# A mixture-of-experts dispatch on one core: loads and stores in one queue, larger transfers, and one broadcast multiply per token

## The chip, the cores and the metric

The kernel runs on one core of a Trainium2 chip. The metric is the device time of one execution in microseconds; lower is better. The kernel before takes 94.59 us (median of 3 runs, 94.53 to 94.8). The span in the profile is shorter, 92.7 us, because it begins with the first and ends with the last recorded instruction.

## The reference

For each of 8 x 256 = 2048 tokens there are a vector x of 512 numbers and 8 gate weights. The weights are divided by their sum, and the output holds x eight times, once per expert, multiplied by that expert's weight:

```
x            [8, 256, 512]     float32
gate_weights [8, 256, 8]       float32
gate_weights = gate_weights / (sum(gate_weights, axis=-1) + 1e-8)
output       [8, 256, 8, 512]  = x[:, :, None, :] * gate_weights[:, :, :, None]
```

The input is 4.26 MB and the output 33.55 MB.

## The kernel before, in words

The 2048 tokens lie over P = 128 partitions, J = 16 consecutive tokens to a partition. One token's output is E x D = 8 x 512 numbers, 16 KB in a partition, and what one partition stores for m tokens is one contiguous run of m x 16 KB in memory.

**Loads.** All gate weights go to `g_all` in one transfer (L54, SyncE's queue). x goes to one tile, `x_all`, in three transfers: tokens 0 and 1 (L55, ScalarE's queue), tokens 2 to 8 (L56, SyncE's queue) and tokens 9 to 15 (L57, ScalarE's queue). No input is loaded later.

**Weights.** VectorE sums the eight weights of each token (L64), takes the reciprocal (L66; the 1e-8 is left out) and multiplies (L68, the reciprocal broadcast over the experts). The result is `gn`. A small copy on ScalarE (L61) brings in its function table early.

**Multiplies.** `compute_tile` (L72) fills one output tile for m tokens with 8 x m multiplies of 128x512 each, one per token and expert. The first `ACT_SHARE[m]` of them go to ScalarE (6 of 16 for two tokens, 10 of 24 for three; L46), the rest to VectorE (L49).

**Stores.** The 16 tokens go in tiles of 2, 3, 3, 3, 3 and 2. The first tile is stored from SyncE's queue (L84), the others from ScalarE's (L89 and L94), so ScalarE's program holds both multiplies and stores, in order. The last 16 numbers of each partition are copied to a small tile `sent` (L100) and stored from SyncE's queue (L101).

**Buffers and order.** The tile pool has three buffers, so the fourth tile waits until the first store has landed, the fifth for the second, and the sixth for the third. The order on each engine is the order of the program; a framework adds the waits for data and for buffers.

Of the kernel before, what the change touches and what calls it, by code (L numbers as in the profile page):

```python
# [1 line left out]

# [4 lines left out]

ACT_SHARE = {1: 3, 2: 6, 3: 10, 4: 13}
SENT = 16  # L10


@with_exitstack
def kernel(
    ctx: ExitStack,
    tc: tile.TileContext,
    x: bass.AP,
    gate_weights: bass.AP,
    out: bass.AP,
):  # L20
    nc = tc.nc
    P = 128

    B, S, D = x.shape
    E = gate_weights.shape[-1]
    n_tok = B * S
    J = n_tok // P

    fp32 = mybir.dt.float32

    x_v = x.flatten_outer_dims().rearrange("(p j) d -> p j d", p=P)
    g_v = gate_weights.flatten_outer_dims().rearrange("(p j) e -> p j e", p=P)
    out_v = out.rearrange("b s e d -> (b s) e d").rearrange(
        "(p j) e d -> p j e d", p=P
    )
    out_flat = out.rearrange("b s e d -> (b s) (e d)").rearrange(
        "(p j) q -> p (j q)", p=P
    )
    tokq = E * D

    xpool = ctx.enter_context(tc.tile_pool(name="xpool", bufs=1))
    gpool = ctx.enter_context(tc.tile_pool(name="gpool", bufs=1))
    tpool = ctx.enter_context(tc.tile_pool(name="tpool", bufs=3))

    def mul_scalar(o_ap, x_ap, s_ap):
        nc.scalar.mul(out=o_ap, in_=x_ap, mul=s_ap)  # L46

    def mul_vector(o_ap, x_ap, s_ap):
        nc.vector.tensor_scalar_mul(out=o_ap, in0=x_ap, scalar1=s_ap)  # L49

    g_all = gpool.tile([P, J, E], fp32)
    x_all = xpool.tile([P, J, D], fp32)

    nc.sync.dma_start(out=g_all, in_=g_v)  # L54
    nc.scalar.dma_start(out=x_all[:, 0:2, :], in_=x_v[:, 0:2, :])  # L55
    nc.sync.dma_start(out=x_all[:, 2:9, :], in_=x_v[:, 2:9, :])  # L56
    nc.scalar.dma_start(out=x_all[:, 9:J, :], in_=x_v[:, 9:J, :])  # L57

    warm = gpool.tile([P, 1], fp32)
    nc.vector.memset(warm, 0.0)  # L60
    nc.scalar.copy(out=warm, in_=warm)  # L61

    gsum = gpool.tile([P, J, 1], fp32)
    nc.vector.reduce_sum(out=gsum, in_=g_all, axis=mybir.AxisListType.X)  # L64
    rsum = gpool.tile([P, J, 1], fp32)
    nc.vector.reciprocal(out=rsum, in_=gsum)  # L66
    gn = gpool.tile([P, J, E], fp32)
    nc.vector.tensor_tensor(  # L68
        out=gn, in0=g_all, in1=rsum.to_broadcast([P, J, E]), op=mybir.AluOpType.mult
    )  # L70

    def compute_tile(pool, j0, m):  # L72
        o_tile = pool.tile([P, m, E, D], fp32)
        n_act = ACT_SHARE[m]
        k = 0
        for jj in range(m):
            for e in range(E):
                mul = mul_scalar if k < n_act else mul_vector
                mul(o_tile[:, jj, e, :], x_all[:, j0 + jj, :], gn[:, j0 + jj, e : e + 1])
                k += 1  # L80
        return o_tile

    tile_p0 = compute_tile(tpool, 0, 2)
    nc.sync.dma_start(out=out_v[:, 0:2, :, :], in_=tile_p0)  # L84

    for t in range(4):
        j0 = 2 + 3 * t
        o_tile = compute_tile(tpool, j0, 3)
        nc.scalar.dma_start(out=out_v[:, j0 : j0 + 3, :, :], in_=o_tile)  # L89

    j0 = J - 2
    last_tile = compute_tile(tpool, j0, 2)
    lf = last_tile.rearrange("p a e d -> p (a e d)")
    nc.scalar.dma_start(  # L94
        out=out_flat[:, j0 * tokq : J * tokq - SENT],
        in_=lf[:, 0 : 2 * tokq - SENT],
    )

    sent = gpool.tile([P, SENT], fp32)
    nc.scalar.copy(out=sent, in_=lf[:, 2 * tokq - SENT : 2 * tokq])  # L100
    nc.sync.dma_start(out=out_flat[:, J * tokq - SENT : J * tokq], in_=sent)  # L101


# [1 line left out]
_INS = ['x', 'gate_weights']  # L105
_OUTS = [((8, 256, 8, 512), 'float32')]


# [23 lines left out]
```

## Time and profile before

| | |
|---|---|
| time | 94.59 us (94.53 to 94.8) |
| span | 92.7 us |
| VectorE busy | 31.4 us, 34% of the span |
| ScalarE busy | 34.0 us, 37% of the span |
| read from HBM, written | 4.26 MB, 33.55 MB |
| mean rate over the span | 408 GB/s |
| one multiply on ScalarE, on VectorE | 707 ns, 480 ns |

Times are in us from the start of the span. In the lines of the profile, DVE is VectorE, ACT is ScalarE, POOL is GpSimd and SP is SyncE; a name with a q behind it (SPq, ACTq) is that engine's sequencer, which issues transfers. L49 is line 49 of the kernel. A row of 40 digits shows the busy share of 40 equal slices of the span in tenths. In groups, `o_tile<-x_all,gn` says what is written and what is read, x76 how often.

### The profile page before, as it was taken

Reading aid. Unit: us, or ns where it says so; the run is one execution under the profiler, and the core shown is the slowest. Engines: PE = TensorE matmul, PEld = TensorE weight load, DVE = VectorE, ACT = ScalarE, POOL = GpSimd, SP = SyncE. Lnnn points to the kernel's source line nnn. Section 1 sums busy time; section 2 is a strip of 40 time slices with the busy share of each in tenths; the row PEclk is TensorE's granted clock in tenths of the full one; section 3 lists DMA queues with packets and bytes.
Section 4 is the critical chain, followed back from the end, with each engine's and each line's share of the span. In section 5 each row is a group of like instructions: output and inputs, shape, how many; then the busy total and the mean of one; then the engine's idle time right before and its main releaser. Section 6 shows DMA issues by size and latency. Waiting matters only on the chain.

```text
span 92.7 us, 204 instructions
## 1 busy us (share of the span) xinstructions
DVE 31.4 (34%) x80; ACT 34.0 (37%) x55; POOL 0.2 (0%) x4
## 2 busy tenths in 40 slices
DVE  0199008999999300399000097000000000000000
ACT  2378008999999910399200096000000000000000
POOL 0000000000000000000000000000000000000000
DMA  1999999999879989988998898899889988999980
GB/s 23 423 402 451 414 350 438 452 452 537 382 339 551 445 360 403 572 382 343 509 466 382 382 572 360 385 445 531 361 361 531 446 382 360 487 451 409 409 367 0
DMA packets 1586, 37.83 MB, mean 408 GB/s; under 512 B 304, under 2 KB 432, under 8 KB 560
## 3 DMA queue, kind: packets, MB, share of 16 engines
q10 hardware_dynamic: 1008, 31.71, 79.8%
q1 hardware_dynamic: 576, 6.10, 15.9%
q14 instruction: 2, 0.02, 0.0%
HBM read 4.26 MB, written 33.55 MB: 408 GB/s over the span
## 4 chain that ended last, share of the span: by engine, by line
DMA 43%; ACT 12%; DVE 4%; issue 1%; DVEq 0%; SPq 0%
DMA out_dram<-o_tile 29%; DMA x_all<-in_x_dram 14%; ACT o_tile L46 12%; DVE o_tile L49 4%; DVEq L127 0%; SPq L54 0%; ACT sent L100 0%; DVEq L49 0%
## 5 line engine op out<-in xcount | busy, mean ns | idle before, releaser
L46 ACT ACTIVATE o_tile<-x_all,gn 128x512 f32<-128x512 f32 x52 | 32.3, 707 | 21.6 <-DMA out_dram<-o_tile 14.3
L49 DVE TENSOR_SCALAR o_tile<-x_all,gn 128x512 f32<-128x512 f32 x76 | 30.5, 480 | 21.8 <-DMA out_dram<-o_tile 16.7
L61 ACT ACT_TABLE_LOAD x1 | 1.3, 1283 | 1.6 <-PEq L116 1.6
L64 DVE TENSOR_REDUCE gsum<-g_all 128x16 f32<-128x128 f32 x1 | 0.3, 286 | 3.4 <-DMA g_all<-in_gate_weights_dram 3.4
L100 ACT COPY sent<-o_tile 128x16 f32<-128x16 f32 x1 | 0.2, 204 | 0.4 <-DVE o_tile L49 0.4
L60 DVE MEMSET warm<- 128x1 f32 x1 | 0.1, 59 | 0.8 <-PEq L116 0.8
L68 DVE TENSOR_TENSOR gn<-g_all,rsum 128x128 f32<-128x128 f32 x1 | 0.3, 293 | 0.0
L66 DVE RECIPROCAL rsum<-gsum 128x16 f32<-128x16 f32 x1 | 0.3, 253 | 0.0
L61 ACT COPY warm<-warm 128x1 f32<-128x1 f32 x1 | 0.2, 191 | 0.0
L116 POOL MEMSET const-bfloat16-1.0<- 128x1 bf16 x1 | 0.1, 102 | 0.0
L116 POOL MEMSET const-uint8-127<- 128x1 uint8 x1 | 0.1, 102 | 0.0
L116 POOL MEMSET const-float32-0.0<- 128x1 f32 x1 | 0.1, 99 | 0.2 <-issue 0.2
L116 POOL MEMSET const-float32-1.0<- 128x1 f32 x1 | 0.1, 99 | 0.0
## 6 DMA issues: line engine op xcount, KB each, us to landing
out_dram<-o_tile ACTq DMA_DIRECT2D x4, 6144.0 KB, 27.8
out_dram<-o_tile SPq DMA_DIRECT2D x1, 4096.0 KB, 14.7
out_dram<-o_tile ACTq DMA_DIRECT2D x1, 4088.0 KB, 34.4
x_all<-in_x_dram ACTq DMA_DIRECT2D x1, 1792.0 KB, 13.2
x_all<-in_x_dram SPq DMA_DIRECT2D x1, 1792.0 KB, 13.0
x_all<-in_x_dram ACTq DMA_DIRECT2D x1, 512.0 KB, 3.9
g_all<-in_gate_weights_dram SPq DMA_DIRECT2D x1, 64.0 KB, 3.5
out_dram<-sent SPq DMA_DIRECT2D x1, 8.0 KB, 18.6
```

Of the source, the lines that this page charges most:

```text
L46: nc.scalar.mul(out=o_ap, in_=x_ap, mul=s_ap)
L49: nc.vector.tensor_scalar_mul(out=o_ap, in0=x_ap, scalar1=s_ap)
L60: nc.vector.memset(warm, 0.0)
L61: nc.scalar.copy(out=warm, in_=warm)
L64: nc.vector.reduce_sum(out=gsum, in_=g_all, axis=mybir.AxisListType.X)
L66: nc.vector.reciprocal(out=rsum, in_=gsum)
L68: nc.vector.tensor_tensor(out=gn, in0=g_all, in1=rsum.to_broadcast([P, J, E]), op=mybir.AluOpType.mult)
L100: nc.scalar.copy(out=sent, in_=lf[:, 2 * tokq - SENT : 2 * tokq])
L116: nc = _bacc.Bacc("TRN2", target_bir_lowering=False, num_devices=1)
```

## The change

It brings the work into one buffer and one queue:

- **Queues.** `g_all` is loaded from ScalarE's queue, and x from SyncE's in two transfers (5 and 11 tokens instead of 2, 7 and 7). All stores are issued from SyncE's queue, so that ScalarE's program holds no store.
- **Larger transfers.** The tokens go in chunks of 2, 3, 3, 4 and 4 (`CHUNKS`: first token, number of tokens, first slot), five stores instead of six. The split-off of the last 16 numbers is dropped.
- **Ten token slots.** In place of three buffers there is one tile `ring` with ten slots of one token each. Chunks 1 to 3 take slots 0-1, 2-4 and 5-7; chunk 4 takes slots 0-3, and chunk 5 slots 6-9. Slots 8 and 9 are used only once.
- **Multiplies.** Tokens 0 and 1 are split as before, three experts of each on ScalarE and five on VectorE. From token 2 on, the first token of each chunk is ScalarE's (eight multiplies), and each other token is one `tensor_tensor` on VectorE over 8 x 512 elements, with x broadcast over the experts and the weights over the 512 elements (`scale_token`).
- **1e-8.** It is added to the sum with one more operation on VectorE, as in the reference.

```diff
--- before.py
+++ after.py
@@ -1,4 +1,3 @@
-
 from contextlib import ExitStack
 
 import concourse.bass as bass
@@ -6,8 +5,9 @@
 from concourse import bass_utils, mybir
 from concourse._compat import with_exitstack
 
-ACT_SHARE = {1: 3, 2: 6, 3: 10, 4: 13}
-SENT = 16
+SLOTS = 10
+HEAD = 5
+CHUNKS = ((0, 2, 0), (2, 3, 2), (5, 3, 5), (8, 4, 0), (12, 4, 6))
 
 
 @with_exitstack
@@ -23,82 +23,70 @@
 
     B, S, D = x.shape
     E = gate_weights.shape[-1]
-    n_tok = B * S
-    J = n_tok // P
+    J = B * S // P
 
     fp32 = mybir.dt.float32
+    mult = mybir.AluOpType.mult
 
     x_v = x.flatten_outer_dims().rearrange("(p j) d -> p j d", p=P)
     g_v = gate_weights.flatten_outer_dims().rearrange("(p j) e -> p j e", p=P)
     out_v = out.rearrange("b s e d -> (b s) e d").rearrange(
         "(p j) e d -> p j e d", p=P
     )
-    out_flat = out.rearrange("b s e d -> (b s) (e d)").rearrange(
-        "(p j) q -> p (j q)", p=P
-    )
-    tokq = E * D
 
-    xpool = ctx.enter_context(tc.tile_pool(name="xpool", bufs=1))
-    gpool = ctx.enter_context(tc.tile_pool(name="gpool", bufs=1))
-    tpool = ctx.enter_context(tc.tile_pool(name="tpool", bufs=3))
+    pool = ctx.enter_context(tc.tile_pool(name="pool", bufs=1))
 
-    def mul_scalar(o_ap, x_ap, s_ap):
-        nc.scalar.mul(out=o_ap, in_=x_ap, mul=s_ap)
+    g_all = pool.tile([P, J, E], fp32)
+    x_all = pool.tile([P, J, D], fp32)
+    ring = pool.tile([P, SLOTS, E, D], fp32)
+    gsum = pool.tile([P, J, 1], fp32)
+    gn = pool.tile([P, J, E], fp32)
+    warm = pool.tile([P, 1], fp32)
 
-    def mul_vector(o_ap, x_ap, s_ap):
-        nc.vector.tensor_scalar_mul(out=o_ap, in0=x_ap, scalar1=s_ap)
+    nc.scalar.dma_start(out=g_all, in_=g_v)
+    nc.sync.dma_start(out=x_all[:, 0:HEAD, :], in_=x_v[:, 0:HEAD, :])
+    nc.sync.dma_start(out=x_all[:, HEAD:J, :], in_=x_v[:, HEAD:J, :])
 
-    g_all = gpool.tile([P, J, E], fp32)
-    x_all = xpool.tile([P, J, D], fp32)
-
-    nc.sync.dma_start(out=g_all, in_=g_v)
-    nc.scalar.dma_start(out=x_all[:, 0:2, :], in_=x_v[:, 0:2, :])
-    nc.sync.dma_start(out=x_all[:, 2:9, :], in_=x_v[:, 2:9, :])
-    nc.scalar.dma_start(out=x_all[:, 9:J, :], in_=x_v[:, 9:J, :])
-
-    warm = gpool.tile([P, 1], fp32)
     nc.vector.memset(warm, 0.0)
     nc.scalar.copy(out=warm, in_=warm)
 
-    gsum = gpool.tile([P, J, 1], fp32)
     nc.vector.reduce_sum(out=gsum, in_=g_all, axis=mybir.AxisListType.X)
-    rsum = gpool.tile([P, J, 1], fp32)
-    nc.vector.reciprocal(out=rsum, in_=gsum)
-    gn = gpool.tile([P, J, E], fp32)
+    nc.vector.tensor_scalar_add(out=gsum, in0=gsum, scalar1=1e-8)
+    nc.vector.reciprocal(out=gsum, in_=gsum)
     nc.vector.tensor_tensor(
-        out=gn, in0=g_all, in1=rsum.to_broadcast([P, J, E]), op=mybir.AluOpType.mult
+        out=gn, in0=g_all, in1=gsum.to_broadcast([P, J, E]), op=mult
     )
 
-    def compute_tile(pool, j0, m):
-        o_tile = pool.tile([P, m, E, D], fp32)
-        n_act = ACT_SHARE[m]
-        k = 0
-        for jj in range(m):
-            for e in range(E):
-                mul = mul_scalar if k < n_act else mul_vector
-                mul(o_tile[:, jj, e, :], x_all[:, j0 + jj, :], gn[:, j0 + jj, e : e + 1])
-                k += 1
-        return o_tile
+    def scale_one(engine, j, e, slot):
+        o_ap, s_ap = ring[:, slot, e, :], gn[:, j, e : e + 1]
+        if engine is nc.scalar:
+            nc.scalar.mul(out=o_ap, in_=x_all[:, j, :], mul=s_ap)
+        else:
+            nc.vector.tensor_scalar_mul(out=o_ap, in0=x_all[:, j, :], scalar1=s_ap)
 
-    tile_p0 = compute_tile(tpool, 0, 2)
-    nc.sync.dma_start(out=out_v[:, 0:2, :, :], in_=tile_p0)
+    def scale_token(j, slot):
+        nc.vector.tensor_tensor(
+            out=ring[:, slot, :, :],
+            in0=x_all[:, j : j + 1, :].to_broadcast([P, E, D]),
+            in1=gn[:, j, :].unsqueeze(2).to_broadcast([P, E, D]),
+            op=mult,
+        )
 
-    for t in range(4):
-        j0 = 2 + 3 * t
-        o_tile = compute_tile(tpool, j0, 3)
-        nc.scalar.dma_start(out=out_v[:, j0 : j0 + 3, :, :], in_=o_tile)
-
-    j0 = J - 2
-    last_tile = compute_tile(tpool, j0, 2)
-    lf = last_tile.rearrange("p a e d -> p (a e d)")
-    nc.scalar.dma_start(
-        out=out_flat[:, j0 * tokq : J * tokq - SENT],
-        in_=lf[:, 0 : 2 * tokq - SENT],
-    )
-
-    sent = gpool.tile([P, SENT], fp32)
-    nc.scalar.copy(out=sent, in_=lf[:, 2 * tokq - SENT : 2 * tokq])
-    nc.sync.dma_start(out=out_flat[:, J * tokq - SENT : J * tokq], in_=sent)
+    for j0, m, s0 in CHUNKS:
+        for i in range(m):
+            j, slot = j0 + i, s0 + i
+            if j < 2:
+                for e in range(E):
+                    on_act = e < 3
+                    scale_one(nc.scalar if on_act else nc.vector, j, e, slot)
+            elif i == 0:
+                for e in range(E):
+                    scale_one(nc.scalar, j, e, slot)
+            else:
+                scale_token(j, slot)
+        nc.sync.dma_start(
+            out=out_v[:, j0 : j0 + m, :, :], in_=ring[:, s0 : s0 + m, :, :]
+        )
 
 
 # ---- launch: one core; inputs and outputs as the reference has them ----
```

## The prediction

> **What bounds the kernel now.** I read the page's totals and slices first, to see which resource is full, then the DMA share by stage, to find where it isn't, and last the opening in order of time.
>
> ```profile
> span 92.7 us, 204 instructions
> ...
> DVE 31.4 (34%) x80; ACT 34.0 (37%) x55; POOL 0.2 (0%) x4
> ...
> DMA  1999999999879989988998898899889988999980
> ...
> HBM read 4.26 MB, written 33.55 MB: 408 GB/s over the span
> ```
>
> No engine is busy more than 37% of the span, but the DMA row is at 8 or 9 tenths nearly from end to end. The kernel is bound by moving 37.83 MB, which the change leaves as it is. What can change is how much of the span the transfers run below their best rate. So, by stage (span and length, busy time of each engine, TensorE clock, DMA share, GB/s):
>
> ```profile
> core 0: us, DVE busy (x) ACT busy (x) POOL busy (x), PEclk, DMA share, GB/s
> ...
> 1.50:2.00 0.50, 0.00 (x0) 0.35 (x1) 0.00 (x0) 1.00 0.21 36
> 2.00:3.00 1.00, 0.00 (x0) 0.99 (x2) 0.00 (x0) 1.00 0.81 224
> 3.00:4.20 1.20, 0.00 (x0) 0.13 (x1) 0.00 (x0) 1.00 1.17 469
> 4.20:10.50 6.30, 4.88 (x13) 3.78 (x6) 0.00 (x0) 1.00 1.02 437
> 10.50:13.00 2.50, 0.00 (x0) 0.00 (x0) 0.00 (x0) 1.00 1.03 328
> 13.00:24.00 11.00, 9.78 (x25) 9.78 (x16) 0.00 (x0) 1.00 1.02 442
> ...
> 53.20:90.00 36.80, 4.05 (x10) 3.99 (x7) 0.00 (x0) 1.00 1.00 433
> 90.00:92.70 2.70, 0.00 (x0) 0.00 (x0) 0.00 (x0) 1.00 0.06 24
> ```
>
> From 13 us to 90 us the stores run at 433 GB/s, with nothing to win. The losses are four. (a) 1.75 us before the first byte. (b) The opening: 0.81 MB moved by 4.20 us, which at 437 GB/s is 1.84 us of the 2.45 us since 1.75: 0.6 us lost. (c) A hollow at 10.5 to 13.0, where loads end and stores begin: 328 instead of 437 GB/s over 2.5 us, 0.6 us lost. (d) The end: 2.7 us with almost nothing moving, in which the last DMA engines finish, the completion arrives and the program closes. Now the opening in order of time (start, length, instruction):
>
> ```profile
> 0.73 0.38 SPq L54 DMA_DIRECT2D g_all<-in_gate_weights_dram  x1
> ...
> 4.22 0.29 DVE L64 TENSOR_REDUCE gsum<-g_all 128x16 f32<-128x128 f32 x1 [3.36 <-DMA g_all<-in_gate_weights_dram]
> ...
> 4.83 0.29 DVE L68 TENSOR_TENSOR gn<-g_all,rsum 128x128 f32<-128x128 f32 x1
> 5.15 3.78 ACT L46 ACTIVATE o_tile<-x_all,gn 128x512 f32<-128x512 f32 x6 [2.02 <-DVE gn L68]
> 5.15 4.05 DVE L49 TENSOR_SCALAR o_tile<-x_all,gn 128x512 f32<-128x512 f32 x10
> 9.30 0.35 SPq L84 DMA_DIRECT2D out_dram<-o_tile  x1
> ```
>
> The first store is issued at 9.30, well before the loads end (14.2, by the first multiply that waits for `x_all`). So nothing ever runs dry; every later store is queued with transfers still ahead of it. The long waits of the engines confirm it: they are waits for buffers, behind a full DMA.
>
> ```profile
> DVE o_tile L49 <- DMA out_dram<-o_tile: 16.7, 2, 9.1
> ACT o_tile L46 <- DMA out_dram<-o_tile: 14.3, 2, 8.5
> ```
>
> **What the Trainium skill says.** (1) "DMA: Bandwidth & Descriptors", section "Where 436 GB/s comes from": a ceiling of 435 GB/s; the stores' 433 agrees. (2) The same page, "Issuing engines are not separate DMA queues": transfers from different engines share the same 16 DMA engines. The trace agrees: 437 GB/s with two queues (4.2 to 10.5 us), 433 with one (53.2 to 90). So one queue for all stores is worth nothing by itself. (3) The same page, "Queues, rings and completion order": a DMA engine takes turns between queues packet by packet. The trace agrees: the 64 KB of `g_all` took 3.5 us to land, nearly as long as the 512 KB of x beside it (3.9).
>
> **The change, part by part.**
>
> *First loads.* `g_all` moves to ACT's queue, and the x load beside it grows from 512 to 1280 KB, in packets 2.5 times as long. If `g_all` still takes turns with it, it lands later by the added 768 KB: 0.786 MB / 433 GB/s = 1.8 us, at 6.0 instead of 4.22. Bounds: 4.2 if its small packets get ahead, 6.9 if it falls one turn behind and waits for a 22 KB packet of the second x load (a sixteenth of 433 is 27 GB/s, so 0.83 us). I take 6.1. The five tokens of x land at 0.73 + 3.9 + 1.8 = 6.4, before they are needed.
>
> *The added 1e-8.* One VectorE operation on 128x16, on the way to `gn`. Not in the trace; between the memset's 0.06 us and the reduction's 0.32 us from start to start. I take 0.3. From `g_all` to the first multiply is 0.93 now (5.15 - 4.22), so 1.2 then: `gn` at 7.3.
>
> *Tokens 0 and 1.* The same 6 multiplies on ScalarE and 10 on VectorE: 4.05 us and 0.1 to the issue. First store issued at 11.45, 2.15 us later than now (bounds 9.7 and 12.3).
>
> *The hand-over from loads to stores.* The transfers issued at 0.73 began to move near 1.75, so an issue into an empty queue takes about 1.0 us: stores could move from 12.5. The loads are done at 1.75 + 0.6 (loss b, kept) + 4.26 MB / 437 GB/s = 12.1. So the wait of 2.15 us is paid almost wholly by the slack that the loads cover, and 0.4 us of idle DMA stands in place of the hollow's 0.6. That is -0.2. If stores are queued before the loads end, the hollow may stay: 12.7, no gain.
>
> *Engine spread at the end.* The hollow also sends the 16 DMA engines into the stores at different moments, and nothing evens them out: in the trace's records the 16 completions of the last store come from 90.6 to 91.9 us, 91.0 on average, so the slowest engine costs 0.9. Engines that start the stores together after a short pause finish closer together. I take -0.4 (bounds 0 and -0.7).
>
> *The split of the last 8 KB (`sent`).* Removed: a copy of 0.2 us and 128 packets of 64 B; the copy lies 34 us before the end, and the packets cost at most -0.1.
>
> *Broadcast multiplies.* For 10 tokens one `tensor_tensor` of 4096 elements replaces eight multiplies. "VectorE: DVE Perf Modes", section "The TRN2 errata", gives (N + 151) / 0.96 ns for an fp32 `tensor_tensor`; for L68's N = 128 that is 291, and the trace has 293, with a broadcast operand. For N = 4096: 4.42 us (estimate). Now eight TENSOR_SCALAR take 8 x 0.405 = 3.24 us, so VectorE loses 1.2 us a token; its total rises from 31 to about 49 us, ScalarE's falls to 38 x 0.63 = 24. The bound from the trace alone would be L68's 293 ns per 128 elements, 9.4 us. I take 4.42. What hides it is the store ahead: chunk 2 needs two (8.9 us; ScalarE's token, 5.0 us, goes beside), while the store of chunk 1 moves 4.19 MB in 9.7 us. Margin 0.8 us, the smallest of all. Chunk 3 comes 8.9 us after chunk 2, behind a store of 14.5 us.
>
> *Ten slots.* Chunk 4 takes slots 0 to 3; its token in slot 2 waits for store 2, which lands near 37.5; two multiplies later, near 46.5, it is issued, and store 3 runs until 51.2. Chunk 5's slots 6 and 7 wait for store 3 (52); behind them in VectorE's order stand the tokens of slots 8 and 9: 13.3 us, issued near 65.5; store 4 runs until 70.6. Margins 4 to 5 us, so nothing on the path. Store issues no longer interrupt ScalarE (0.46 us each), which has room anyway.
>
> **Sum:** -0.2 (hand-over), -0.4 (spread), -0.1 (`sent`): -0.7 us, 93.9.
>
> **Rivals.**
> A. *No change:* the hollow comes with any hand-over, or the store arrives just as late as the loads used to end; the engines' spread stays. For it: all edits but the opening lie behind a full DMA. Against: the hollow falls where loads and a queued store overlap. 94.5.
> B. *A gap at the hand-over:* `g_all` falls behind, the store is issued at 12.3 and moves at 13.4 or later, 0.7 to 1.5 us after its place now. For it: the opening chain grows by over 2 us and the slack is about as long. Against: it needs the late bound twice. 95.5, slower.
> C. *The broadcast multiply is slower than its price:* at 6 us, chunk 2 is late by 2 x 1.6 - 0.8 = 2.4 us, and chunk 5 by some tenths: 97. Against: L68 fits the price.
> D. *The ring is tracked as one buffer,* so each chunk's compute waits for the store before: 8.9 + 8.9 + 13.3 + 13.3 us and some 2 us each time come bare: near 145. Against: token 0 starts at 5.15 while two other loads into `x_all` are under way, so parts of a tile are told apart.
>
> **How the numbers follow.** Forecast 0.6; A 0.2; B 0.11, C 0.06, D 0.03. The forecast's own spread is 93.2 (no idle at the hand-over, full gain of the spread) to 94.3; A ends at 94.8; up to 95.1 takes in part of B. The range 93.2 to 95.1 leaves out C, D and the worse half of B. Faster 0.6, same 0.2, slower 0.2.
>
> **What would show it.** Right: VectorE's first operation near 6.1 us; first store issued near 11.5; the windows after 13 us at 433 GB/s with no idle; TENSOR_TENSOR at 4.4 us; the chain ending in DMA alone; less than 2.7 us of quiet at the end. Wrong: a dip of the DMA row near 12 us longer than 0.6 us (B), or near 22 us (C), or before each store (D).

## The result and the profile after

The changed kernel takes 93.67 us (median of 4 runs, 93.55 to 93.77), beside 94.69 for the kernel before on the same chip (its three runs above and one more): a ratio of 0.989 (95% interval 0.987 to 0.991). It is faster by 1.0 us, 1.1%. The page of the changed kernel:

```profile
span 92.0 us, 131 instructions
...
DVE 48.6 (53%) x25; ACT 25.1 (27%) x40; POOL 0.2 (0%) x4
...
DMA  3899989999777977997797999999972999999990
...
q1 hardware_dynamic: 1008, 37.75, 95.8%
q10 hardware_dynamic: 144, 0.07, 0.3%
HBM read 4.26 MB, written 33.55 MB: 411 GB/s over the span
```

The bound is the same: DMA nearly full, VectorE now busy for half of the span and still free. The isolated low digits late in the DMA row are the long packets being counted where they begin (a 64 KB packet lasts more than a slice); no engine runs dry there. Two things are less plain. There are 131 instructions instead of 204, and the list of DMA queues has two rows. In the kernel before it has a third, which the prediction read over:

```profile
q10 hardware_dynamic: 1008, 31.71, 79.8%
q1 hardware_dynamic: 576, 6.10, 15.9%
q14 instruction: 2, 0.02, 0.0%
```

Two packets of 8 KB of instructions, fetched through the same DMA engines while the stores run. They carry 0.04% of the bytes; the experiments show that they cost far more than that.

The stages of the changed kernel, cut as before:

```profile
core 0: us, DVE busy (x) ACT busy (x) POOL busy (x), PEclk, DMA share, GB/s
...
2.00:3.00 1.00, 0.00 (x0) 0.62 (x2) 0.00 (x0) 1.00 0.41 159
3.00:4.20 1.20, 0.00 (x0) 0.00 (x0) 0.00 (x0) 1.00 1.04 422
4.20:10.50 6.30, 3.58 (x11) 2.58 (x5) 0.00 (x0) 1.00 1.03 437
10.50:13.00 2.50, 2.50 (x5) 2.50 (x5) 0.00 (x0) 1.00 1.04 446
...
53.20:90.00 36.80, 3.62 (x1) 4.20 (x7) 0.00 (x0) 1.00 0.99 427
90.00:92.70 2.70, 0.00 (x0) 0.00 (x0) 0.00 (x0) 1.00 0.00 0
```

The hollow of 328 GB/s at 10.5 to 13.0 us is gone (part of the 446 is long packets counted at their start). After 90 us no packet starts, where the kernel before still moved 24 GB/s. The opening in order of time:

```profile
6.78 0.29 DVE L53 TENSOR_REDUCE gsum<-g_all 128x16 f32<-128x128 f32 x1 [5.92 <-DMA g_all<-in_gate_weights_dram]
7.10 0.17 DVE L54 TENSOR_SCALAR gsum<-gsum 128x16 f32<-128x16 f32 x1
7.31 0.25 DVE L55 RECIPROCAL gsum<-gsum 128x16 f32<-128x16 f32 x1
...
7.92 4.05 DVE L65 TENSOR_SCALAR ring<-x_all,gn 128x512 f32<-128x512 f32 x10
11.88 39.10 DVE L68 TENSOR_TENSOR ring<-x_all,gn 128x4096 f32<-128x4096 f32 x9
12.06 45.70 SPq L87 DMA_DIRECT2D out_dram<-ring  x5
```

The weights arrive 2.6 us later than before and the first store goes out at 12.06 instead of 9.30: the chain that leads to the first store grew by 2.8 us, and the kernel got faster. The trace's DMA records show how. They list every packet with its start, length and size but not its engine; how far the 16 engines are apart is read from the last 16 load packets, the first 16 packets of a store, and the 16 completions of a transfer. The 16 DMA engines finish their loads at 12.5 us on average (13.2 before), stand idle for 0.45, and begin the stores within 0.15 us of each other (12.91 to 13.06; before, 12.81 to 13.91). At the end the 16 completions of the last store come at 91.02 to 91.18, mean 91.09. In the kernel before it was 90.58 to 91.89, mean 91.02. **The average engine finishes no earlier than before; only the slowest does, by 0.7 us.** The profiled spans differ by as much (92.7 and 92.0); the medians differ by 1.0 us, so 0.3 us of the gain isn't in these two profiles.

### The profile page after: what moved, and what is told of

It reads as the page before. It is cut to its first block, busy times and chain, and to the rows that moved or that the text cites. A ratio compares the mean times of both kernels' runs of the same rounds, so it can differ in the third digit from the quotient of the medians.

```text
span 92.0 us, 131 instructions
## 1 busy us (share of the span) xinstructions
DVE 48.6 (53%) x25; ACT 25.1 (27%) x40; POOL 0.2 (0%) x4
## 3 DMA queue, kind: packets, MB, share of 16 engines
HBM read 4.26 MB, written 33.55 MB: 411 GB/s over the span
## 4 chain that ended last, share of the span: by engine, by line
DMA 31%; DVE 23%; ACT 5%; issue 2%; ACTq 1%; SPq 0%
DMA out_dram<-ring 25%; DVE ring L68 17%; DMA g_all<-in_gate_weights_dram 7%; ACT ring L63 5%; DVE ring L65 4%; ACTq L115 1%; DVE gn L56 0%; DVE gsum L53 0%; DVE gsum L55 0%; DVE gsum L54 0%; ACTq L63 0%; SPq L87 0%
## 5 line engine op out<-in xcount | busy, mean ns | idle before, releaser
L68 DVE TENSOR_TENSOR ring<-x_all,gn 128x4096 f32<-128x4096 f32 x10 | 43.5, 4417 | 1.4 <-DMA out_dram<-ring 1.4
L63 ACT ACTIVATE ring<-x_all,gn 128x512 f32<-128x512 f32 x38 | 23.6, 709 | 31.2 <-DMA out_dram<-ring 25.9
L65 DVE TENSOR_SCALAR ring<-x_all,gn 128x512 f32<-128x512 f32 x10 | 4.0, 482 | 0.0
## 6 DMA issues: line engine op xcount, KB each, us to landing
x_all<-in_x_dram SPq DMA_DIRECT2D x1, 2816.0 KB, 12.1
```

The costliest lines, as they stand in the source:

```text
L63: nc.scalar.mul(out=o_ap, in_=x_all[:, j, :], mul=s_ap)
L65: nc.vector.tensor_scalar_mul(out=o_ap, in0=x_all[:, j, :], scalar1=s_ap)
L68: nc.vector.tensor_tensor(out=ring[:, slot, :, :], in0=x_all[:, j : j + 1, :].to_broadcast([P, E, D]), in1=gn[:, j, :].unsqueeze(2).to_bro ...
```

## The experiments

All ratios are to the kernel before, run on the same chip in the same series, where it took 94.82 to 94.85 us; times are medians. The changed kernel itself ran only beside the four runs of the result (94.69), so a difference from its 93.67 is uncertain by some 0.2 us.

**The loads alone.** The loads of the kernel before are replaced by the three of the changed kernel.

```diff
-    nc.sync.dma_start(out=g_all, in_=g_v)
-    nc.scalar.dma_start(out=x_all[:, 0:2, :], in_=x_v[:, 0:2, :])
-    nc.sync.dma_start(out=x_all[:, 2:9, :], in_=x_v[:, 2:9, :])
-    nc.scalar.dma_start(out=x_all[:, 9:J, :], in_=x_v[:, 9:J, :])
+    nc.scalar.dma_start(out=g_all, in_=g_v)
+    nc.sync.dma_start(out=x_all[:, 0:5, :], in_=x_v[:, 0:5, :])
+    nc.sync.dma_start(out=x_all[:, 5:J, :], in_=x_v[:, 5:J, :])
```

> The kernel before with the loads of the changed kernel alone (g_all on ScalarE's queue, x in 5 and 11 tokens on SyncE's); multiplies, six stores, their queues and the split of the last 8 KB stay. Theory: the loads alone carry the whole gain, 93.6 to 93.9, first store issued near 11.8, spread of the last completions under 0.4 us. Rival 1 (larger store transfers, fewer instructions, no split): most of the gain missing, 94.3 or more.

Measured: 94.13 us, ratio 0.992 (0.988 to 0.995). It lies between the two expectations: the loads carry most of the gain, not all. The records say why. First store at 11.67, engines within 0.23 us at the start of the stores, and 0.2 us apart when the first two stores land; then, when the third lands, one engine is 1.0 us behind, and stays so. The page again has the row for instructions:

```profile
span 92.3 us, 202 instructions
...
q14 instruction: 2, 0.02, 0.0%
```

Its first packet is at 42.7 us, between the landing that is even (37.3) and the one that isn't (51.8 to 52.8). At the end the slowest engine is 0.74 us behind the mean, hardly less than the 0.87 of the kernel before, and the profiled span is 0.4 us shorter, where the median fell by 0.7. So part of what the new loads win is in executions that have no trace; the experiments with the store held back come to it again.

**The broadcast multiply undone.** In the changed kernel the same tokens are VectorE's, by eight multiplies each.

```diff
-                scale_token(j, slot)
+                for e in range(E):
+                    scale_one(nc.vector, j, e, slot)
```

> The changed kernel with the broadcast multiply undone: the same tokens on VectorE, but by eight multiplies of 128x512 each (8 x 0.405 = 3.2 us a token instead of 4.42), 70 instructions more. Theory: VectorE is hidden behind the stores either way, 93.7 and no difference, at most 0.3 us more where an instruction fetch delays one DMA engine. Rival 1 (fewer instructions carry the gain): slower by 0.4 us or more.

Measured: 94.24 us, ratio 0.993 (0.991 to 0.996), 0.57 more than the changed kernel, or 0.4 by the two ratios. The theory named no more than 0.3; the rival's 0.4 or more came. VectorE does less (37.0 us busy instead of 48.6) and the kernel is slower. It has 201 instructions and one instruction packet, at 24.8 us; by the next landing one DMA engine is 0.9 us behind the rest. So the multiply matters by its number of instructions or by how it uses the engine. The next experiments part the two.

**Instructions that do nothing, among the multiplies.** Nine multiplies of 128x1 behind each of eight broadcast multiplies; `pad` is a new tile of one number per partition, which nothing reads.

```diff
                 scale_token(j, slot)
+                if j >= 6:
+                    for e in range(9):
+                        nc.vector.tensor_scalar_mul(
+                            out=pad, in0=ring[:, slot, E - 1, D - 1 : D], scalar1=1.0)
```

> The changed kernel with nine VectorE multiplies of 128x1 added behind each of eight broadcast multiplies (72 instructions more on VectorE, as many as the kernel without broadcast has; they write a number that nothing reads). Theory (an instruction fetch of 8 KB that falls among the stores holds up one of the 16 DMA engines, and nothing makes up for it): the transfer row of instructions, absent in the changed kernel, shows one packet; one DMA engine lands 0.7 to 0.9 us behind the others; 94.1 to 94.4 against 93.67. Rival (the kernel without broadcast was slower for its multiplies' way of using VectorE or SBUF): no fetch needed, 93.6 to 93.8.

Measured: 98.18 us, ratio 1.035 (1.032 to 1.039). This was badly placed. The framework put 24 of them, 4.5 us, ahead of the last two tokens of chunk 4, and that store was issued at 55.55, when the one before it had ended:

```profile
42.30 4.49 DVE L90 TENSOR_SCALAR pad<-ring 128x1 f32<-128x1 f32 x24
46.71 8.76 DVE L69 TENSOR_TENSOR ring<-x_all,gn 128x4096 f32<-128x4096 f32 x2
55.55 0.33 SPq L93 DMA_DIRECT2D out_dram<-ring  x1
...
DMA  3899999997977977977970099999999999999990
```

The two empty slices behind 51 us are a real hole, 4.7 us in the DMA records (51.7 to 56.4), as long as the added work and no shorter. So chunk 4 has nothing to spare, where the prediction gave it 4 us. In the changed kernel its store is issued at 51.06, and the records have a gap of 0.12 us there. And one instruction packet fell at 52.0, leaving one engine 1.2 us behind; after the hole all 16 landed within 0.2 us again. A pause evens the engines.

**The same instructions at the end.** 72 of them behind VectorE's last broadcast multiply, where nothing follows.

```diff
+    for e in range(72):
+        nc.vector.tensor_scalar_mul(
+            out=pad, in0=ring[:, 7, E - 1, D - 1 : D], scalar1=1.0)
```

> The changed kernel with 72 VectorE multiplies of 128x1 behind its last broadcast multiply; they write a number that nothing reads, nothing is queued behind them, and they are over long before the stores end. Theory (a fetch of instructions among the stores holds up one DMA engine): one packet in the transfer row of instructions, one DMA engine landing 0.7 to 0.9 us behind the others, 94.1 to 94.4. Rival (the kernel without broadcast lost its time in the multiplies themselves): 93.6 to 93.8, as the changed kernel.

Measured: 94.63 us, ratio 0.999 (0.997 to 1.000), nearly 1.0 us more than the changed kernel (0.9 by the two ratios), above what the theory had. The page and VectorE's last work:

```profile
span 92.7 us, 203 instructions
...
q14 instruction: 1, 0.01, 0.0%
```

```profile
52.19 4.43 DVE L69 TENSOR_TENSOR ring<-x_all,gn 128x4096 f32<-128x4096 f32 x1 [1.40 <-DMA out_dram<-ring]
56.65 13.56 DVE L92 TENSOR_SCALAR pad<-ring 128x1 f32<-128x1 f32 x72
```

VectorE is done at 70 us, 20 us before the stores. No engine and no store waits for these instructions. One packet of 8 KB, 0.31 us long, falls at 64.2; the store landing at 52 us is even to 0.2 us, the next has one engine 1.0 us behind the mean, and the last has one 0.9 behind; the other 15 end within 0.2 us. The records also say how 0.31 us becomes 0.9: the store packet that ends where this packet begins lasted 2.72 us and the one that begins where it ends 2.77, beside 2.43 for the others. Why these two take longer is not shown. VectorE itself wasn't held up: its 72 instructions start every 187 to 190 ns, also at 64.2. So the cost of the 72 instructions is that of their fetch, and it is shown.

**The broadcast multiply alone.** In the kernel before, tiles from token 5 on give their first token to ScalarE and every other to one broadcast multiply.

```diff
-        n_act = ACT_SHARE[m]
+        n_act = ACT_SHARE[m] if j0 < 5 else E
...
+            if j0 >= 5 and jj > 0:
+                nc.vector.tensor_tensor(out=o_tile[:, jj, :, :], ...)
+                continue
```

> The kernel before with the broadcast multiply alone: in the tiles from token 5 on, the first token of a tile is ScalarE's and every other is one broadcast multiply on VectorE; loads, queues, buffers, six stores and the split stay. Theory: no instruction fetch among the stores; the engines still come 1.1 us apart out of the loads, so the slowest gains only what the fetches added to it: 94.3 to 94.8 against 94.85. Rival (the hand-over alone carries the gain): 94.85, no difference.

Measured: 94.25 us, ratio 0.995 (0.993 to 0.997), just below the range expected, and against the rival. The theory had no instruction packet among the stores; one is left, at 57.5 us, where ScalarE's program ends, with 51 recorded instructions on ScalarE. The slowest engine ends 0.68 us behind the mean. The two parts alone multiply to 0.986, beside 0.989 for the whole change.

**Why the loads help: the store held back.** Two attempts. The first put a long memset on VectorE ahead of the reciprocal:

```diff
+    idle = gpool.tile([P, 2600], fp32)
+    nc.vector.memset(idle, 0.0)
```

> The kernel before, with one edit: a VectorE memset of 2600 elements (about 2.7 us) between the sum and the reciprocal, so that the first store is issued near 12.1 us instead of 9.30, when the loads are almost done. Theory (the gain of the change is the hand-over: a store queued behind two running load queues slows the last loads and sends the 16 DMA engines into the stores apart; a short pause starts them together): although the chain grows by 2.7 us, the kernel gets faster by 0.5 to 1.0 us, near 93.8; no hollow at 10.5 to 13 us, and the last store's completions within 0.3 us. Rival 1 (the gain comes from larger transfers, fewer instructions or the dropped split): same time as before or slower by up to 0.5 us, 94.6 to 95.1. Rival 2 (the hollow comes with any end of two load queues): hollow stays, 94.5 or more.

Measured: 94.93 us, ratio 1.002 (1.000 to 1.004), but nothing had been held: the memset (2.23 us long) had been moved into the wait for `g_all`, and the first store was issued at 8.69. It leaves one number. Slow load packets begin at 10.05, 1.36 us after that issue; in the kernel before at 10.65, 1.35 us after its own (and in the one with the broadcast multiply alone at 10.07, 0.86 after). The second attempt puts the delay into the chain itself:

```diff
+    wide = gpool.tile([P, J, 180], fp32)
+    nc.vector.tensor_tensor(
+        out=wide, in0=gsum.to_broadcast([P, J, 180]),
+        in1=gsum.to_broadcast([P, J, 180]), op=mybir.AluOpType.max)
-    nc.vector.reciprocal(out=rsum, in_=gsum)
+    nc.vector.reciprocal(out=rsum, in_=wide[:, :, 179:180])
```

> The kernel before with a VectorE operation of 2880 elements (about 3.1 us) put into the chain from the sums to the reciprocals, so that nothing can be moved ahead of it: the first store is issued near 12.4 us instead of 9.30. Theory (a store that comes while two load queues run slows the loads; in the kernel before the slow packets begin 1.35 us after its issue): the loads run undisturbed to their end near 12.4, no hollow before the store, the engines begin the stores together; 94.1 to 94.5, as in the kernel with the new loads alone, although the first store is issued 3 us later. Rival 1 (the hollow comes with the end of two load queues): slow packets between 10.6 and 13 stay, 94.9 to 95.8. Rival 2 (the time is set by when the first store starts): 95 or more.

Measured: 94.85 us, ratio 1.000 (0.998 to 1.002). The store was issued at 11.79, and in the profile the mechanism is as the theory has it:

```profile
10.50:12.00 1.50, 1.20 (x4) 0.93 (x2) 0.00 (x0) 1.00 0.98 421
```

No hollow although two load queues end there, so rival 1 is out; the engines begin the stores within 0.15 us, and the first two land 0.2 us apart. Two instruction packets (42.8 and 59.1 us) then leave one engine 0.75 us behind the mean. But the time missed the expectation, and rival 2's 95 is hardly missed: holding the store won nothing in the median. Its profiled execution was the quickest of its 22 (94.32); what the others lost isn't in a trace.

So both causes were taken away in the kernel before: the store held, and broadcast multiplies from token 5 on, with 38 multiplies on ScalarE.

> The kernel before with two things at once: the first store held back by a 2880-element operation in the chain of the weights, and the broadcast multiply for the tokens from 5 on (ScalarE has 38 multiplies as in the changed kernel). Loads in two queues, three buffers, stores from ScalarE's queue, six stores and the split stay. Theory (held store and few instructions are the two causes, and the held store alone gave nothing because two instruction fetches hid it): no hollow, no fetch, last completions within 0.3 us, 93.6 to 94.0. Rival (the new load queues matter beyond the moment of the first store): 94.4 or more.

Measured: 94.37 us, ratio 0.994 (0.992 to 0.997). The profiled execution (93.77, again the quickest, of 11) is as expected: no hollow, no instruction packet among the stores, completions within 0.2 us. The median is 0.6 us above it, outside the theory's 93.6 to 94.0 and 0.03 short of the rival, and no better than that of the broadcast multiply alone (94.25). The executions without traces say a little more. With the loads of the kernel before, the median lies 0.3 to 0.7 us above the quickest execution (in the kernel before and four variants of it, with 11 to 59 executions); with the new loads, or `g_all` ahead of x in one queue, it lies 0.03 to 0.23 above (up to 22 executions). This points to something in the old loads, apart from the moment of the first store, that costs most executions some tenths of a microsecond; what it is stays open.

**A store queued earlier.** The changed kernel with `g_all` first on SyncE's queue: once with the loads as they are, and once with x in three loads, the first of two tokens.

```diff
-    nc.scalar.dma_start(out=g_all, in_=g_v)
+    nc.sync.dma_start(out=g_all, in_=g_v)
```

> The changed kernel with one edit: g_all is loaded from SyncE's queue, ahead of x. The weights come near 3 us instead of 6.75, so the first five tokens of x (landing near 6.6) set the first store: issued near 10.7 instead of 12.06, with about 2 us of loads still to come. Theory: no idle DMA between loads and stores, but the engines enter the stores as they finish their loads, 0.6 us apart; if the hollow is the store queued behind running loads, it returns and the time is 94.2 to 94.6. If the hollow needs two load queues, it doesn't return and the time falls to 93.1 to 93.5, since the slowest engine's loads ended at 12.9 and its stores began at 13.06. Rival 1: no difference, 93.7.

Measured: 93.64 us, ratio 0.986 (0.982 to 0.990): no change against the changed kernel, as the rival had it. The store, issued at 11.21, follows the loads without idle time, and there is no hollow. But x is issued 0.43 us later, its loads end 0.4 us later (12.9 on average), and the engines keep the 0.6 us by which they left the loads.

```diff
-    nc.scalar.dma_start(out=g_all, in_=g_v)
-    nc.sync.dma_start(out=x_all[:, 0:HEAD, :], in_=x_v[:, 0:HEAD, :])
+    nc.sync.dma_start(out=g_all, in_=g_v)
+    nc.sync.dma_start(out=x_all[:, 0:2, :], in_=x_v[:, 0:2, :])
+    nc.sync.dma_start(out=x_all[:, 2:HEAD, :], in_=x_v[:, 2:HEAD, :])
```

> The changed kernel with g_all first in SyncE's queue and x in three loads there (tokens 0 and 1, 2 to 4, 5 to 15), so that the first store is issued near 9.2 us, 3 us before the loads end, in the same single queue. Theory (the hollow needs a store in another queue's way; behind loads of its own queue a store waits its turn): no slow load packets, no idle DMA, and the stores follow without a gap; 93.3 to 93.6. Rival (any store that is queued while loads run slows them): load packets slow from 10.5 us on as in the kernel before, 94.0 to 94.4.

Measured: 94.56 us, ratio 0.998 (0.996 to 1.000); the rival was right. The store was issued at 8.96, and from 1.26 us later the loads look so:

```profile
8.96 0.35 SPq L88 DMA_DIRECT2D out_dram<-ring  x1
...
10.20:13.50 3.30, 3.30 (x2) 3.30 (x6) 0.00 (x0) 1.00 1.08 328
```

All of it is in one queue, so the hollow has nothing to do with two queues. Load packets that take 836 ns in the changed kernel take 840 to 1000 here before that and up to 1700 after it, and the loads end at 13.95 on average (12.9 in the kernel with the gates first and two x loads). So a store that is queued while loads still run slows those loads, in four kernels from 0.9 to 1.4 us after its issue. Where the last load packets had begun by 1.4 us after it (the changed kernel with the gates first, and the one below), none was slow. Why a store does so is not shown. A smaller part of the delay comes from elsewhere: until 10.2 us, too, these loads ran at 426 GB/s, not 437.

**The store a little earlier.** If a store does harm only from about 1.3 us after its issue, it should be issued about that long before the loads end (at 12.5), not 0.45 us before.

```diff
-HEAD = 5
+HEAD = 4
```

> The changed kernel with four tokens of x in the first load instead of five. The weights share the DMA engines with 256 KB less, so the first store comes 0.4 to 0.6 us earlier, near 11.5. Theory (0.45 us of idle DMA between loads and stores, and a store slows loads only from some 1.3 us after its issue): the idle time goes, no slow loads, 93.2 to 93.5. Rival (the engines then start the stores as far apart as they finish the loads, 0.6 us, which takes the gain back): 93.6 to 93.8.

Measured: **92.88 us**, ratio 0.980 (0.977 to 0.984), the best version, and better than expected. The weights come at 5.88 and the store is issued at 11.16.

```profile
11.16 45.88 SPq L87 DMA_DIRECT2D out_dram<-ring  x5
...
10.50:12.00 1.50, 1.50 (x3) 1.50 (x4) 0.00 (x0) 1.00 1.06 459
12.00:13.00 1.00, 1.00 (x1) 1.00 (x3) 0.00 (x0) 1.00 1.22 524
```

No load packet is slow, no engine idles: loads end at 12.37 on average, stores begin at 12.38. The engines enter the stores 0.36 us apart, and the last completions are within 0.17 us all the same: chunk 4's store is issued at 50.16, the early engines wait for it, and that evens them. The stores also take 77.5 us, beside 77.8 in the changed kernel, whose 16 engines run in step from the start with slightly longer packets (32 KB in 1224 ns, not 1213).

**Smaller stores.** The chunks of the changed kernel as 2, 3, 3, 3, 3 and 2 tokens, six stores of at most 6 MB. ScalarE has eight multiplies more, and VectorE one broadcast multiply less.

```diff
-CHUNKS = ((0, 2, 0), (2, 3, 2), (5, 3, 5), (8, 4, 0), (12, 4, 6))
+CHUNKS = ((0, 2, 0), (2, 3, 2), (5, 3, 5), (8, 3, 0), (11, 3, 3), (14, 2, 8))
```

> The changed kernel with chunks of 2, 3, 3, 3, 3 and 2 tokens instead of 2, 3, 3, 4 and 4: six stores of at most 6 MB, in the same ten slots and the same queue. Theory: the DMA engines are as full with 48 KB to a partition as with 64 KB, 93.6 to 93.8. Rival (larger transfers carry part of the gain): 94.0 or more.

Measured: 93.79 us, ratio 0.989 (0.986 to 0.992). The larger transfers carry nothing that shows.

## Why the prediction was right, and where it wasn't

The time lay 0.2 us below the forecast, on the forecast's side. That it came so near is partly luck: in the profile the forecast's sum of -0.7 us came about as +0.07 for the hand-over and -0.78 for the spread, and one of the two causes of the spread was not in the forecast. By its steps:

- **The bound and the 433 GB/s.** Right: 431 GB/s from 13 to 90 us in the changed kernel, 434 in the kernel before. The forecast compared two queues of loads with one queue of stores; that one queue is enough for the loads of x too is now seen, with 437 GB/s from 4.2 to 10.5 us in both kernels.
- **First loads.** Weights at 6.1 forecast, 6.78 measured, just within the late bound of 6.9. The mechanism (small packets taking turns with longer ones) holds in direction: with 256 KB less in the first load they came 0.9 us earlier, where the added bytes at 433 GB/s give 0.6. The forecast left out that the first, longer packets start more slowly (159 GB/s between 2 and 3 us, not 224).
- **The 1e-8.** 0.21 us from start to start (7.10 to 7.31), 0.3 forecast.
- **First store.** 12.06, not 11.45: the 0.7 us by which the weights were late, less 0.1.
- **The hand-over, -0.2.** The loads end at 12.5 us on average, where 12.1 was forecast; the idle time is 0.45 us (0.4 forecast). On average an engine begins its stores 0.2 us earlier than before (12.97 against 13.16), as forecast. It is then given back: the engines that start in step need 0.3 us more for their stores. Net on the average engine's completion: +0.07.
- **The spread, -0.4.** The mis-sized term, and the whole gain in the profile: the slowest engine was 0.87 us behind the mean and is now 0.09 behind, 0.78 less, where the bound was 0.7. The step named one cause, the uneven entry into the stores, and it is in the records: in the kernel before the last engine begins its stores 0.75 us behind the mean, and with the store held or late the engines start within 0.25 us. It missed the other, the instruction packets. The two don't add up: with the entry even and the packets left, the slowest engine still ends 0.74 or 0.75 behind (the loads alone, the store held); with the packets fewer and the entry uneven, 0.68 (the broadcast multiply alone); only with both gone about 0.1 (the changed kernel, and the kernel before with both). In the medians the even entry alone is not shown to win anything: with the store held they did not fall.
- **Broadcast multiplies.** The duration was right: 4.42 us estimated from the Trainium skill's page "VectorE: DVE Perf Modes", and

```profile
L68 DVE TENSOR_TENSOR ring<-x_all,gn 128x4096 f32<-128x4096 f32 x10 | 43.5, 4417 | 1.4 <-DMA out_dram<-ring 1.4
```

  It is hidden but for 0.12 us (below). But "hidden" was taken for "worth nothing", and this is the step that failed: the multiply takes 70 instructions out of VectorE's program, and the new split of the tokens takes ScalarE's from 55 to 40, and with them go the instruction packets among the stores. Undoing the multiply costs 0.4 to 0.6 us; adding 72 idle instructions at the end costs 0.9 to 1.0. The Trainium skill, "Runtime: NRT & Kernel Launch", section "Instruction fetch mechanics", calls the cost of a refill mostly hidden. For the engine that executes the instructions that agrees with the trace (72 starts at 187 to 190 ns without a break); for the DMA engine that brings them it doesn't: 0.31 us of packet, 0.9 to 1.0 us of delay.
- **Ten slots.** Margins of 4 to 5 us were forecast; chunk 4 had none. The forecast took VectorE's tokens in the order of the program. The framework put the two of chunk 5's free slots 8 and 9 ahead of the two of chunk 4 that wait for slots, 8.8 us, so store 4 was issued at 51.06 instead of 46.5, and 0.12 us of idle DMA is the result; the last store went out at 57.43, not 65.5:

```profile
29.23 21.76 DVE L68 TENSOR_TENSOR ring<-x_all,gn 128x4096 f32<-128x4096 f32 x5
51.06 0.33 SPq L87 DMA_DIRECT2D out_dram<-ring  x1
```

  VectorE so has nine broadcast multiplies back to back and waits 1.4 us in all. A kernel with tokens 14 and 15 kept behind chunk 4 was not tried.
- **`sent`, -0.1.** Not told apart by any run.
- **Rivals.** A's mechanism, a hollow that stays in one queue too, exists (the kernel with the store at 8.96), but in the changed kernel the store came too late for it. B's gap is the 0.45 us of idle time, no more. C and D did not occur.

## What to carry to other kernels

In a kernel that is bound by DMA, look at the slowest of the 16 DMA engines and not at their mean: what delays one of them early is carried to the end, unless a pause evens it. Fewer instructions can pay although every compute engine is idle half the time, because their fetches run through the same DMA engines; look for a row of instruction packets in the list of queues. And try the first store at several moments: with the gates first in one queue, a store issued at 8.96 instead of 11.21 cost 0.9 us; with the gates in their own queue, one at 12.06 instead of 11.16, 1.2 us before the loads end, cost 0.8. Each step also changed the cut of the first loads.

## What the runs showed of the hardware

- One packet of 8 KB of instructions among the stores puts one DMA engine 0.9 to 1.2 us behind where the engines were even before it, though the packet itself takes 0.31 us (93.67 to 94.63 us for the kernel, by 72 instructions); the store packets just before and after it take 0.3 us longer each (2.72 and 2.77 us instead of 2.43). In the kernels here that had one among the stores, an engine's program held 51 recorded instructions or more; in those that had none, 48 or fewer (the changed kernel has 25 on VectorE and 40 on ScalarE).
- A store that is queued behind running loads slows them from 0.9 to 1.4 us after its issue, before it moves a byte itself: 328 instead of 437 GB/s, with one queue as with two.
- Sixteen engines that start in step run slightly slower than when they are some tenths of a microsecond apart: 77.7 to 77.9 us in the seven kernels whose engines start within 0.23 us (without the one with the hole), beside 77.3 to 77.5 in the six others, for the same 33.55 MB. A packet of the first store, 32 KB, takes 1220 to 1225 ns beside 1213. Why is not shown.
